# A hybrid decoder layer on one core: the order of the first tiles, of the first input projection weights, and of the last weights

## The chip, the cores and the metric

The kernel runs on one core of one Trainium2 chip. The metric is the device time of one execution in microseconds (us). Engines: TensorE (PE; PEld is its weight load), VectorE (DVE), ScalarE (ACT), GpSimd (POOL), and SyncE (SP), which issues most DMA transfers. Each engine runs its instructions in order; semaphores tie them together.

## The reference

One layer, with S = 512 tokens, D = 1024, feed-forward width 2816, and RMS norms around every sub-layer:

```
h = x + 0.5 * post(swiglu1(pre(x)))            # w_gu 1024 x 5632, w_down 2816 x 1024
z = pre(h) @ W_in + b_in                       # 2304 columns: two mixers' heads
h += post(concat(A, B) @ W_out + b_out)        # A: window + sinks, B: dilated windows
h += 0.5 * post(swiglu2(pre(h)))
h += post(sigmoid(pre(h) @ W_gate) * (p @ W_ple))   # the "gate" stage
```

All is fp32. Token mixing is causal.

## The kernel before, in words

**Operands.** Each fp32 operand is kept as two halves: a high half, which is a ScalarE cast to fp32r (`L197`), and a low half, the source minus the high half (`L198`). A product of two operands is three TensorE products: high x high, high x low, low x high, all issued in `mm` (`L96`). `prep` (`L183`) loads one weight of 128 x 1024 through SP's queue into one of four raw buffers, casts it, and subtracts it. The subtraction runs on `state["lo"]`, which is VectorE or GpSimd.

**Tokens.** The 512 tokens are four tiles t = 0 to 3. `pre` normalises a tile: a Square with its row sum on ScalarE (`L296`), two small GpSimd instructions (`L297`, `L298`), and a scale on VectorE (`L310`). `post` ends a sub-layer with `L320` and `L321` on VectorE. `transpose_x` turns a tile with eight TensorE transposes (`L330`), and makes its high half on ScalarE (`L336`) and its low half on VectorE (`L337`), in two parts of 512 columns each.

**Stages.** ffn1's gate and up products run first; the very first blocks take only the columns of tiles 0 and 1 (256), so that they can start before tiles 2 and 3 are there. Then come ffn1's down products, which use operand slots named "a", "c" and "B" for each block pair, and inside it `e_tile` (a part of the per-layer embedding: products, then a ScalarE copy `L439` into a raw buffer and an SP store `L441`). The seam from ffn1's down products to the attention's input projection has first the four value tiles `v_b(0)` to `v_b(3)` (their weights are "vb"), each with the transposes of the next token tile in its middle, and then the "z" columns. After attention, output projection and ffn2 the gate stage takes tile by tile; its eight weights `("gate", k)` are loaded as slots come free. A tile's columns are computed in parts of 512; the last tile's in 512, 256 and 256. Each part is followed by a chain on ScalarE (`L1124`), VectorE (`L1125`, `L1128`, `L1134`), and after the last part by GpSimd (`L1137`) and the final VectorE step `L1139` with the output's store.

**What sets the order.** TensorE's order is that of the code. At the start the code fixes ScalarE's and VectorE's order as well (`in_order`); elsewhere a scheduler with priorities orders ScalarE, VectorE, GpSimd and SP. `todo` is the list of weights to come, `free` the list of slots, and `release(key)` gives a slot back and lets `pump` prepare the next weight in it.

Of the kernel before, what the change touches and what calls it, by code (L numbers as in the profile page):

```python
# [55 lines left out]
def hybrid_layer(ctx: ExitStack, tc: tile.TileContext, x, p, rel_bias, ffn1_pre_g, ffn1_w_gu, ffn1_w_down,  # L56
# [3 lines left out]
    nc = tc.nc  # L60
# [140 lines left out]
    todo = []  # L201
# [250 lines left out]
            nc.tensor.transpose(PS[:, 0, 0:P], ident, ident)  # L452

    state["first"] = True
    xts = [load_h(0, x)]
    g_pre = bcast(1, ffn1_pre_g)
    xts.append(load_h(1, x))
    warm(24)
    xss = {}
    with in_order():  # L460
        xss[0] = pre(0, xts[0], g_pre, buf("x"))
        prep(todo.pop(0), free.pop(0))
        xss[1] = pre(1, xts[1], g_pre, buf("x"))
        xts.append(load_h(2, x))
        for t in range(2):
            transpose_x(t, xss.pop(t), t)
        prep(todo.pop(0), free.pop(0))
        xss[2] = pre(2, xts[2], g_pre, buf("x"))
    xts.append(load_h(3, x))
    pump()  # L470
    xss[3] = pre(3, xts[3], g_pre, buf("x"))

    def ffn(n, wait_tr, after_first):

# [33 lines left out]
    def down(n, extra, finish, between):  # L508
# [43 lines left out]
        def m7(m, i, e=False):  # L552
            product(C11, i, W[("B" + n, m)], 256, W[("a" + n, m)], 512, False, e)

        def done(m):
            for k in "acB":
                release((k + n, m))
        for fs in ((m3, m2), (m7, m6)):
            for m in range(2):
# [10 lines left out]
        for t in range(2):  # L570
            for f in (m3, m7):
                for m in last:
                    f(m, t, m == NPAIR - 1)
            with tc.high_priority():
                nc.scalar.copy(q[t], C12[t])
            finish(t)
            for m in last:
                m2(m, t, m == NPAIR - 1)
            with tc.high_priority():
                nc.vector.tensor_tensor(q[t], q[t], C21[t], op=ALU.subtract)  # L580
                nc.vector.tensor_tensor(C22[t], C22[t], q[t], op=ALU.add)
        for t in range(2):
            e_tile(n, t)
            if t == 1:
                between(2)
            for m in last:
                m6(m, t, m == NPAIR - 1)
            if t == 1:
                for m in last:
                    done(m)  # L590
            finish(2 + t)
        release(("ple", 0))
        release(("ple", 1))
# [44 lines left out]
    def first_extra():  # L638
        for a in slots1:
            retire(a)  # L640
        assert not todo
        lower(F32R, "heads")
        for j in range(4):
            prep(("vb", j), half_slot(flat(cur["t"]), 1 + j))
        state["lo"] = nc.gpsimd
        todo.extend([("z", f) for f in (QB, KB, QB + 1, KB + 1, QB + 2, KB + 2, QB + 3, KB + 3, KA, VA, 0, 1, 2, 3)])
        todo.extend([("o", f) for f in (6, 7, 0, 1)])

    xss = {}

# [10 lines left out]
    state["first"] = False  # L661


    state["lo"] = nc.gpsimd

    def first(fn):
        def run(*a):
# [37 lines left out]

    v_b(0, lambda: transpose_x(1, xss.pop(1), 1))
    v_b(1, lambda: transpose_x(2, xss.pop(2), 2))
    v_b(2, lambda: transpose_x(3, xss.pop(3), 3))
    v_b(3)
    W.pop(("vb", 0)), W.pop(("vb", 1)), W.pop(("vb", 2)), W.pop(("vb", 3))  # L710
    g_post = bcast(0, attn_post_g)
    g_pre = bcast(1, ffn2_pre_g)
# [394 lines left out]
    for t in range(NT):  # L1107
        ps = flat(slot2(t))
        cols = slice(t * P, (t + 1) * P)
        y, h = ybuf[t], load_h(t)  # L1110
        last = t == NT - 1
        parts = [slice(0, 512), slice(512, 768), slice(768, 1024)] if last else [slice(0, 512), slice(512, 1024)]
        total = None
        for n, c in enumerate(parts):
            o = PS[:, 0, 0:256] if n == 2 else ps[:, c]
            for k in range(NK):
                wh, wl = W[("gate", k)]
                mm(o, XH[:, k, cols], wh[:, c], k == 0, False)
                mm(o, XH[:, k, cols], wl[:, c], False, False)
            if t < 3 and n == 0:  # L1120
                transpose_x(t + 1, xss.pop(t + 1), t + 1)
            for k in range(NK):
                mm(o, XL[:, k, cols], W[("gate", k)][0][:, c], False, k == NK - 1)
            nc.scalar.activation(y[:, c], o, AF.Sigmoid)  # L1124
            nc.vector.tensor_tensor(y[:, c], y[:, c], es[t][:, c], op=ALU.mult)  # L1125
            ms = col()
            if last:
                nc.vector.tensor_tensor_reduce(out=o, in0=y[:, c], in1=y[:, c], scale=1.0 / D,  # L1128
                                               scalar=EPS if n == 0 else total, op0=ALU.mult, op1=ALU.add,
                                               accum_out=ms)  # L1130
            else:
                nc.scalar.activation(o, y[:, c], AF.Square, scale=1.0 / 32.0, accum_out=ms)
                nc.gpsimd.tensor_scalar(ms, ms, EPS if n == 0 else total, None, op0=ALU.add)
            nc.vector.tensor_tensor(y[:, c], y[:, c], g_ple[:, c], op=ALU.mult)  # L1134
            total = ms
        r = col()
        nc.gpsimd.tensor_tensor(r, total, neghalf, op=ALU.pow)  # L1137
        for c in (slice(0, 512), slice(512, 1024)):
            nc.vector.scalar_tensor_tensor(h[:, c], y[:, c], r, h[:, c], op0=ALU.mult, op1=ALU.add)  # L1139
            nc.sync.dma_start(out[t * P:(t + 1) * P, c], h[:, c])  # L1140
# [35 lines left out]
```

## Time and profile before

| | |
|---|---|
| median of three runs | 1014.91 us (1014.45 to 1017.21) |
| the profiled execution, its own time | 1016.56 us |
| its span in the trace | 1014.8 us |
| TensorE busy | 979.2 us (96%) |
| VectorE, ScalarE, GpSimd busy | 630.6, 431.2, 126.6 us |
| TensorE's mean granted clock | 0.986 of full speed |

The span is what the trace covers of the profiled execution; the time beside it is that execution's own. A matmul's end is modelled, so a busy TensorE need not be at its peak. The views are read as: start, duration, engine, line and operation, output from inputs, and in brackets the idle time ahead with what ended it.

### The profile page before, as it was taken

The numbers are of one execution on the slowest core, as the hardware profiler recorded it, in microseconds if no ns is written. First come the engines' busy times: TensorE is split into PE (matmuls) and PEld (weight loads), VectorE is DVE, ScalarE is ACT, GpSimd is POOL, SyncE is SP. The second block draws the span as 40 slices with busy tenths as digits, with TensorE's granted clock in tenths as the row PEclk, the third lists the DMA queues.
The fourth block names the chain that finished last, engine by engine and source line by source line (L and its number), as shares of the span: only waits on it lengthen the run. The fifth ranks groups of instructions, "written<-read, shape, count | busy, mean of one in ns | idle before, by whom it ended". The sixth has DMA issues, their size and how long they took to land.

```text
span 1014.8 us, 12639 instructions
## 1 busy us (share of the span) xinstructions
PE 979.2 (96%) x4769; PEld 823.3 (81%) x4769; DVE 630.6 (62%) x968; ACT 431.2 (42%) x638; POOL 126.6 (12%) x138
## 2 busy tenths in 40 slices
PE   6999999999999998999988999999999999999897
PEld 6987888888887876888877889888888888878786
DVE  5455554554887686277789684545554639776944
ACT  5332222222556463377777354222222225655641
POOL 2000000000000034232232220000000000000411
PEclk7999999999999999999999999999999999999999
DMA  9577768774465567243232365777668544655741
GB/s 276 146 259 239 244 235 292 226 269 159 132 209 187 176 214 230 84 128 111 84 115 63 115 188 183 250 254 252 226 224 275 210 167 153 205 189 190 277 137 63
DMA packets 147992, 193.71 MB, mean 191 GB/s; under 512 B 5993, under 2 KB 112043, under 8 KB 145115
## 3 DMA queue, kind: packets, MB, share of 16 engines
q1 hardware_dynamic: 138779, 141.00, 44.5%
q0 software_dynamic: 9152, 51.91, 14.0%
q8 instruction: 37, 0.61, 0.2%
q14 instruction: 24, 0.20, 0.1%
HBM read 150.91 MB, written 39.35 MB: 187 GB/s over the span
## 4 chain that ended last, share of the span: by engine, by line
PE 50%; DVE 5%; issue 2%; ACT 2%; DMA 1%; POOL 0%; DVEq 0%; POOLq 0%; SPq 0%; ACTq 0%
PE banks L96 48%; DVE hb L863 1%; PE banks L330 1%; DVE fb L899 1%; DVE fb L888 1%; DMA raw<-sums 0%; DVE hb L755 0%; PE banks L908 0%; ACT heads L753 0%; DVE heads L755 0%; ACT heads L762 0%; ACT wr L197 0%; DVE hb L941 0%; PE banks L826 0%; DVE hb L764 0%
## 5 line engine op out<-in xcount | busy, mean ns | idle before, releaser
L96 PE MATMUL banks<-xh,wr 128*128 128x512 f32 (+1 forms) x1024 | 293.4, 367 | 0.1
L96 PE MATMUL banks<-xh,hb 128*128 128x512 f32 (+1 forms) x872 | 254.4, 374 | 0.0
L96 PEld LDWEIGHTS banks<-xh,wr 128*128 128x128 f32 x1024 | 186.7, 191 | 30.0 <-ACT xh L336 0.5
L96 PE MATMUL banks<-xl,wr 128*128 128x512 f32 (+1 forms) x512 | 187.0, 365 | 0.8 <-DVE xl L337 0.8
L96 PEld LDWEIGHTS banks<-xh,hb 128*128 128x128 f32 x872 | 159.9, 188 | 29.5 <-issue 0.6
L96 PE MATMUL banks<-xl,hb 128*128 128x512 f32 (+1 forms) x436 | 161.5, 373 | 0.0
L197 ACT CAST wr<-raw 128x1024 fp32r<-128x1024 f32 x59 | 62.0, 1052 | 142.0 <-PE banks L96 108.5
L197 ACT CAST hb<-raw 128x1024 fp32r<-128x1024 f32 x50 | 52.7, 1053 | 161.6 <-PE banks L96 147.5
L96 PEld LDWEIGHTS banks<-xl,wr 128*128 128x128 f32 x512 | 98.0, 191 | 15.6 <-DVE xl L337 1.1
L388 DVE TENSOR_TENSOR fb<-fb 128x512 f32<-128x512 f32 x110 | 70.1, 687 | 53.6 <-DMA sums<-fb 47.9
L96 PEld LDWEIGHTS banks<-xl,hb 128*128 128x128 f32 x436 | 82.1, 188 | 14.5
L198 DVE TENSOR_TENSOR hb<-raw,hb 128x1024 fp32r<-128x1024 f32 x50 | 60.8, 1221 | 43.6 <-ACT hb L197 43.4
L362 DVE TENSOR_TENSOR hidden<-hidden,banks 128x512 f32<-128x512 f32 x44 | 30.1, 685 | 64.0 <-PE banks L96 63.3
L198 DVE TENSOR_TENSOR wr<-raw,wr 128x1024 fp32r<-128x1024 f32 x41 | 50.0, 1221 | 30.7 <-ACT wr L197 30.6
L297 POOL TENSOR_SCALAR small<-small 128x1 f32<-128x1 f32 x28 | 17.4, 621 | 339.7 <-ACT fb L296 302.9
L147 ACT CAST hb<-raw 128x1024 fp32r<-128x1024 f32 (+1 forms) x37 | 38.5, 1041 | 44.7 <-PE banks L96 41.4
L198 POOL TENSOR_TENSOR wr<-raw,wr 128x1024 fp32r<-128x1024 f32 x18 | 43.9, 2437 | 103.1 <-ACT wr L197 93.1
L148 DVE TENSOR_TENSOR hb<-raw,hb 128x1024 fp32r<-128x1024 f32 (+1 forms) x37 | 44.6, 1206 | 18.0 <-ACT hb L147 17.5
L96 PE MATMUL banks<-hb,wr 128*128 128x512 f32 x210 | 52.3, 390 | 0.7 <-DVE wr L148 0.7
L148 DVE TENSOR_TENSOR wr<-raw,wr 128x1024 fp32r<-128x1024 f32 (+1 forms) x27 | 32.3, 1199 | 33.0 <-ACT wr L147 33.0
L147 ACT CAST wr<-raw 128x1024 fp32r<-128x1024 f32 (+1 forms) x27 | 27.7, 1036 | 52.3 <-PE banks L96 52.3
L96 PE MATMUL banks<-wr,hb 128*128 128x512 f32 x184 | 48.5, 392 | 0.1
(167 smaller groups left out, 1473.8 us busy)
## 6 DMA issues: line engine op xcount, KB each, us to landing
raw<-in_ffn_w_gu_dram SPq DMA_DIRECT2D x88, 512.0 KB, 4.5
sums<-fb POOLq DMA_DIRECT2D x22, 1280.0 KB, 8.1
fb<-in_ffn_w_down_dram POOLq DMA_DIRECT2D x22, 1024.0 KB, 8.5
raw<-sums SPq DMA_DIRECT2D x44, 512.0 KB, 3.5
raw<-in_w_in_dram SPq DMA_DIRECT2D x18, 512.0 KB, 4.4
raw<-in_ffn_w_down_dram SPq DMA_DIRECT2D x24, 256.0 KB, 2.8
raw<-sums SPq DMA_DIRECT2D x22, 256.0 KB, 3.3
fb<-hd SPq DMA_DIRECT2D x11, 512.0 KB, 6.4
```

What stands on the lines that cost most here:

```text
L96: nc.tensor.matmul(o, l, r, start=start, stop=stop, skip_group_check=loose)
L147: nc.scalar.copy(hi, src)
L148: nc.vector.tensor_tensor(lo, src, f32(hi), op=ALU.subtract)
L197: nc.scalar.copy(hi, raw)
L198: state["lo"].tensor_tensor(lo, raw, f32(hi), op=ALU.subtract)
L297: nc.gpsimd.tensor_scalar(ms, ms, 4 * EPS if half else EPS, None, op0=ALU.add)
L330: nc.tensor.transpose(ps[:, k // 4, (k % 4) * P:(k % 4 + 1) * P], xs[:, k * P:(k + 1) * P], ident)
L362: nc.vector.tensor_tensor(h, h, two(ps[:, 1, :]), op=ALU.mult)
L388: nc.vector.tensor_tensor(o[:, i * 512:(i + 1) * 512], x1, x2, op=op)
L863: nc.vector.tensor_tensor(lo, v, f32(hi), op=ALU.subtract)
L888: nc.vector.tensor_tensor_reduce(out=pi, in0=sview(i)[:, :n], in1=back(tb, 0, n), scale=-0.125, scalar=nsink[:, h:h + 1], op0=ALU.add, op1 ...
L899: nc.vector.tensor_scalar(pi, pi, rs[:, i:i + 1], None, op0=ALU.mult)
```

## The change

It has four parts.

1. At the start, x's tiles 0 and 1 are loaded ahead of the gain `bc`, and both are squared ahead of the first weight's cast. Tiles 2 and 3 are loaded ahead of the third weight, tile 3 into a spare `BC` buffer.
2. The list of "z" weights is filled after `v_b(1)` in the code, no longer within ffn1's down stage, and the first three are prepared there with VectorE as `state["lo"]`; GpSimd takes over from the fourth on.
3. The last blocks' "a" slots are released ahead of the e tiles, "c" and "B" after them as before. This holds for ffn1 and ffn2.
4. The last tile's columns are split 512, 384, 128.

```diff
@@ start
-    xts = [load_h(0, x)]
+    xts = [load_h(t, x) for t in range(2)]
     g_pre = bcast(1, ffn1_pre_g)
-    xts.append(load_h(1, x))
     warm(24)
     xss = {}
     with in_order():
-        xss[0] = pre(0, xts[0], g_pre, buf("x"))
+        for t in range(2):
+            xss[t] = pre(t, xts[t], g_pre, buf("x"))
         prep(todo.pop(0), free.pop(0))
-        xss[1] = pre(1, xts[1], g_pre, buf("x"))
-        xts.append(load_h(2, x))
-        for t in range(2):
-            transpose_x(t, xss.pop(t), t)
+        transpose_x(0, xss.pop(0), 0)
+        transpose_x(1, xss.pop(1), 1)
         prep(todo.pop(0), free.pop(0))
+        xts += [load_h(2, x), load_h(3, x, BC[:, 2, :])]
         xss[2] = pre(2, xts[2], g_pre, buf("x"))
-    xts.append(load_h(3, x))
+        prep(todo.pop(0), free.pop(0))
+        xss[3] = pre(3, xts[3], g_pre, buf("x"))
     pump()
-    xss[3] = pre(3, xts[3], g_pre, buf("x"))
@@ down
-        def done(m):
-            for k in "acB":
+        def done(m, kinds="acB"):
+            for k in kinds:
                 release((k + n, m))
...
+        for m in last:
+            release(("a" + n, m))
         for t in range(2):
             e_tile(n, t)
...
                 for m in last:
-                    done(m)
+                    done(m, "cB")
@@ end of ffn1, value products
-        state["lo"] = nc.gpsimd
-        todo.extend([("z", f) for f in (QB, KB, QB + 1, KB + 1, QB + 2, KB + 2, QB + 3, KB + 3, KA, VA, 0, 1, 2, 3)])
-        todo.extend([("o", f) for f in (6, 7, 0, 1)])
...
-    state["lo"] = nc.gpsimd
...
     v_b(1, lambda: transpose_x(2, xss.pop(2), 2))
+    todo.extend([("z", f) for f in (QB, KB, QB + 1, KB + 1, QB + 2, KB + 2, QB + 3, KB + 3, KA, VA, 0, 1, 2, 3)])
+    todo.extend([("o", f) for f in (6, 7, 0, 1)])
+    for _ in range(3):
+        prep(todo.pop(0), free.pop(0))
+    state["lo"] = nc.gpsimd
     v_b(2, lambda: transpose_x(3, xss.pop(3), 3))
     v_b(3)
+    pump()
@@ gate
-        parts = [slice(0, 512), slice(512, 768), slice(768, 1024)] if last else [slice(0, 512), slice(512, 1024)]
+        parts = [slice(0, 512), slice(512, 896), slice(896, 1024)] if last else [slice(0, 512), slice(512, 1024)]
-            o = PS[:, 0, 0:256] if n == 2 else ps[:, c]
+            o = PS[:, 0, 0:128] if n == 2 else ps[:, c]
```

**The start, ScalarE.** From its first Square on, before the change (`fb` are token buffers, `raw` a loaded weight, `wr` and `hb` its operand slots, `banks` the PSUM, `xh` and `xl` the tiles' halves):

```order
L296 ACTIVATE fb,small<-fb 128x1024
L197 CAST wr<-raw 128x1024
L296 ACTIVATE fb,small<-fb 128x1024
L336 CAST xh<-banks 128x4x128 x2
L197 CAST wr<-raw 128x1024
L336 CAST xh<-banks 128x4x128
L197 CAST wr<-raw 128x1024
```

The same place of ScalarE with the change:

```order
L296 ACTIVATE fb,small<-fb 128x1024 x2
L197 CAST wr<-raw 128x1024
L336 CAST xh<-banks 128x4x128 x4
L197 CAST wr<-raw 128x1024
L296 ACTIVATE fb,small<-fb 128x1024
```

The second Square has moved ahead of the first cast, and all four parts of the two tiles' high halves ahead of the second cast. VectorE's order moves in the same way: both L310 ahead of the first L198, four L337 behind it.

**The seam, VectorE.** From the end of ffn1's down stage to the third value tile, before the change (here `bc` holds the gains, and one token tile too):

```order
L310 SCALAR_TENSOR_TENSOR fb<-fb,small,bc 128x1024 x2
L320 TENSOR_TENSOR fb<-banks,bc 128x1024
L321 SCALAR_TENSOR_TENSOR fb<-fb,small 128x1024
L337 TENSOR_TENSOR xl<-banks,xh 128x4x128 x2
L310 SCALAR_TENSOR_TENSOR fb<-fb,small,bc 128x1024
L320 TENSOR_TENSOR fb<-banks,bc 128x1024
L337 TENSOR_TENSOR xl<-banks,xh 128x4x128 x2
L700 TENSOR_TENSOR fb<-banks,fb 128x512
L321 SCALAR_TENSOR_TENSOR bc<-fb,small,bc 128x1024
L704 TENSOR_TENSOR heads<-fb,heads 128x8x64
```

The same place with the change (its L697 and L701 are L700 and L704 of before):

```order
L310 SCALAR_TENSOR_TENSOR fb<-fb,small,bc 128x1024 x2
L320 TENSOR_TENSOR fb<-banks,bc 128x1024
L321 SCALAR_TENSOR_TENSOR fb<-fb,small 128x1024
L337 TENSOR_TENSOR xl<-banks,xh 128x4x128 x2
L198 TENSOR_TENSOR wr<-raw,wr 128x1024
L310 SCALAR_TENSOR_TENSOR fb<-fb,small,bc 128x1024
L320 TENSOR_TENSOR fb<-banks,bc 128x1024
L198 TENSOR_TENSOR wr<-raw,wr 128x1024
L321 SCALAR_TENSOR_TENSOR bc<-fb,small,bc 128x1024
L337 TENSOR_TENSOR xl<-banks,xh 128x4x128 x2
L697 TENSOR_TENSOR fb<-banks,fb 128x512
L701 TENSOR_TENSOR heads<-fb,heads 128x8x64
```

Two low halves, of z1 and z2 (counted from 0), have come in between tile work, and L321 of the last tile stands ahead of the second tile's L337. The low half of z0 has come in too, some rows earlier, ahead of an L321. GpSimd has lost these three, and its order is otherwise the same. On ScalarE the first copy L439 now stands ahead of the Square that it stood behind.

**The gate stage's begin, ScalarE.** Around the two e tiles of ffn2, before the change:

```order
L296 ACTIVATE fb,small<-banks 128x1024
L197 CAST hb<-raw 128x1024
L296 ACTIVATE fb,small<-fb 128x1024
L439 COPY raw<-banks 128x1024
L296 ACTIVATE fb,small<-fb 128x1024
L296 ACTIVATE fb,small<-banks 128x1024
L439 COPY raw<-banks 128x1024
L336 CAST xh<-banks 128x4x128 x2
L197 CAST wr<-raw 128x1024
L296 ACTIVATE fb,small<-banks 128x1024
L296 ACTIVATE fb,small<-fb 128x1024
L197 CAST hb<-raw 128x1024
```

The same place with the change:

```order
L296 ACTIVATE fb,small<-banks 128x1024
L197 CAST hb<-raw 128x1024 x2
L197 CAST wr<-raw 128x1024
L296 ACTIVATE fb,small<-fb 128x1024
L439 COPY raw<-banks 128x1024
L296 ACTIVATE fb,small<-fb 128x1024
L296 ACTIVATE fb,small<-banks 128x1024
L439 COPY raw<-banks 128x1024
L336 CAST xh<-banks 128x4x128 x2
L296 ACTIVATE fb,small<-banks 128x1024
L296 ACTIVATE fb,small<-fb 128x1024
```

Two casts of gate weights have moved up to the first; on VectorE their low halves have moved with them, ahead of the first tile's L310.

## Rows read from the trace of the kernel before

**Rows 1.** Busy time of the engines over the whole span (first part of the page).

```profile
PE 979.2 (96%) x4769; PEld 823.3 (81%) x4769; DVE 630.6 (62%) x968; ACT 431.2 (42%) x638; POOL 126.6 (12%) x138
```

**Rows 2.** Busy time of each engine in three stretches; PEclk is the granted clock.

```profile
23.00:24.00 1.00, 1.00 (x9) 1.00 (x9) 0.23 (x2) 0.51 (x1) 0.71 (x2) 0.80 1.20 290
50.00:100.00 50.00, 50.00 (x247) 42.26 (x245) 27.61 (x42) 13.09 (x16) 4.20 (x6) 1.00 0.76 248
400.00:402.00 2.00, 2.00 (x6) 1.52 (x6) 0.69 (x1) 0.11 (x1) 0.00 (x0) 0.50 0.99 373
```

**Rows 3.** Timeline of the start, 5 to 18.5 us (start, duration, [idle before <-releaser]).

```profile
6.71 1.28 DVE L310 SCALAR_TENSOR_TENSOR fb<-fb,small,bc 128x1024 f32<-128x1024 f32 x1 [5.85 <-DMA bc<-in_ffn_pre_g_dram]
...
9.71 1.04 ACT L197 CAST wr<-raw 128x1024 fp32r<-128x1024 f32 x1 [4.47 <-DMA raw<-in_ffn_w_gu_dram]
...
10.78 1.23 DVE L198 TENSOR_TENSOR wr<-raw,wr 128x1024 fp32r<-128x1024 f32 x1 [2.79 <-ACT wr L197]
...
14.00 1.28 DVE L337 TENSOR_TENSOR xl<-banks,xh 128x512 fp32r<-128x512 f32 x2
...
14.14 1.97 PE L330 MATMUL banks<-ident,fb 128*128 128x128 f32 x8 [5.00 <-DVE fb L310]
...
17.59 0.58 PE L96 MATMUL banks<-xl,wr 128*128 128x256 f32 x1 [0.80 <-DVE xl L337]
```

**Rows 4.** Timeline of the seam, 368 to 407 us, same columns.

```profile
371.30 0.62 PE L96 MATMUL banks<-xh,hb 128*128 128x512 f32 x2
...
373.91 1.00 ACT L439 COPY raw<-banks 128x1024 f32<-128x1024 f32 x1
...
380.28 0.38 SPq L196 DMA_DIRECT2D raw<-in_w_in_dram  x1
...
381.98 3.50 DVE L310 SCALAR_TENSOR_TENSOR fb<-fb,small,bc 128x1024 f32<-128x1024 f32 x1 [0.98 <-POOL small L298]
...
382.00 2.40 POOL L198 TENSOR_TENSOR wr<-raw,wr 128x1024 fp32r<-128x1024 f32 x1
...
385.88 1.05 ACT L197 CAST wr<-raw 128x1024 fp32r<-128x1024 f32 x1 [2.94 <-DMA raw<-in_w_in_dram]
...
388.19 4.00 PE L96 MATMUL banks<-heads,xh 128*128 128x512 f32 x16 [0.99 <-DVE xl L337]
...
391.54 1.05 ACT L197 CAST wr<-raw 128x1024 fp32r<-128x1024 f32 x1 [3.64 <-DMA raw<-in_w_in_dram]
...
396.38 1.28 DVE L310 SCALAR_TENSOR_TENSOR fb<-bc,small 128x1024 f32<-128x1024 f32 x1 [0.77 <-POOL small L298]
...
398.32 5.54 PE L96 MATMUL banks<-heads,xh 128*128 128x512 f32 x16 [3.38 <-DVE xl L337]
```

**Rows 5.** Timeline of the gate's first tile, 945 to 967 us, same columns.

```profile
950.77 1.27 DVE L310 SCALAR_TENSOR_TENSOR fb<-fb,small,bc 128x1024 f32<-128x1024 f32 x1
...
953.66 1.03 PE L330 MATMUL banks<-ident,fb 128*128 128x128 f32 x8
...
960.53 0.50 PE L96 MATMUL banks<-hb,xh 128*128 128x512 f32 x1 [0.50 <-ACT hb L197]
...
963.20 0.50 PE L96 MATMUL banks<-hb,xh 128*128 128x512 f32 x1 [2.17 <-DVE hb L198]
...
963.54 1.03 PE L330 MATMUL banks<-ident,fb 128*128 128x128 f32 x8
```

**Rows 6.** Timeline of 128-column products and of the tail, same columns.

```profile
458.06 0.22 PE L96 MATMUL banks<-heads,hb 128*128 128x128 f32 x1
...
458.22 0.45 PE L96 MATMUL banks<-xh,wr 128*128 128x512 f32 x1
...
1001.48 1.34 PE L96 MATMUL banks<-gates,xh 128*128 128x256 f32 x10
...
1004.30 1.31 PE L96 MATMUL banks<-gates,xh 128*128 128x256 f32 x10
...
1009.61 1.41 DVE L1139 SCALAR_TENSOR_TENSOR fb<-fb,small 128x512 f32<-128x512 f32 x2 [0.44 <-POOL small L1137]
```

## The prediction

> **What bounds the kernel now.** I read the page's first part, then the windows, then the timeline of every stretch in which TensorE's busy time falls short, engine by engine. TensorE is busy 979.2 of 1014.8 us [rows 1]; in the long stages it has no gap at all at full clock (50.00 of 50 us, [rows 2]). So no edit that only frees another engine's time is worth anything unless it ends one of TensorE's waits, makes TensorE do less, or gives it its clock sooner. The 35.6 us of gaps sit in a few places, and the change touches four: the start, the seam from ffn1's down stage to the value products, the gate's first tile, and the last tile's tail. The sum below is made against the profiled execution, 1016.56 us (span 1014.8 and 1.76 around it); the median of the three runs shown is 1014.91, so 1.65 comes off at the end.
>
> **Start: -3.7.** Now the first product that reads a low half starts at 17.59, held by VectorE's third L337 [rows 3]. That one is the last of a chain: the gain `bc` lets L310 of tile 0 start at 6.71, but L310 of tile 1 stands behind the first low half L198 (10.78) and, on ScalarE, the Square of tile 1 behind the first cast, which waits for the weight's DMA until 9.71. TensorE's transposes of tile 1 follow at 14.14, after 5.00 of waiting. After the change both Squares are done before that cast. The cast itself stays at 9.71: x0, x1, gain and g0 are still the first four loads. The gain is the third now, not the second: it lands no sooner than 6.71 and no later than g0's 9.71; I take the middle, 8.2. Two L310 (1.28 each) end at about 10.8, L198 of g0 (from 10.8, when the cast ends, 1.23) at 12.0, three L337 (0.64 each, half of the 1.28 for two) at 13.9. That is the new start of the low products, 3.7 before 17.59. With the gain at 9.71, two L310 end at 12.3, L198 at 13.5, L337 at 15.4: -2.2. The clock makes the other bound. It comes up in slice 23 to 24 (0.80, [rows 2]), and if it comes up no earlier, the 3.7 us are run at 1.2 GHz and are worth half, -1.9; if it rises as much earlier as the products do, all 3.7, and with the gain landing at 6.71 up to -5. I take 3.7, since the products run without a break from 17.59 on and before them the engine waited. The two x loads that now stand ahead of g1 in SP's queue delay g1 by one load: it lies under g0's and u0's 48 short products. If that cover is gone the price is the length of one load, about 2.4 us (g0, the fourth load, was there at 9.71), inside the range.
>
> **Seam: -3.4.** The change text says that weights wait for the value products, but by the order the loads of the first z weights stand where they did in SP's queue. What moves is two things. On ScalarE the copy of the first e tile (L439) now goes ahead of a Square that waits for VectorE. TensorE's e products end at 371.9 (371.30 and 0.62, [rows 4]), so the copy can run at 372.0, not 373.91: 1.9 earlier. The raw buffer that it feeds from is freed by its store, and the load of z2, at 380.28, waits for that: 378.4; z2's cast, which waits for this DMA, goes from 385.88 to 384.0, z3's from 391.54 to 389.6. And the low halves of z0, z1 and z2 go from GpSimd (2.40 each) to VectorE (1.22). That adds 3 x 1.22 = 3.7 us to VectorE ahead of tile work, and it takes away what GpSimd did to VectorE: L310 at 381.98 took 3.50 beside GpSimd's 2.40 of low half, against 1.28 [rows 4], so one such meeting cost 2.2.
> At the second value tile: z2's cast ends 385.05, L198 1.22, L321 1.28 (the same size as L310), first L337 0.64, which is 388.2, against 388.19 now: nothing gained or lost, any gain upstream ends in this wait. At the third: z3's low half stays on GpSimd ahead of the norm of tile 3, so the chain from z3's cast (391.54) over L310 (396.38) to the products (398.32) keeps its 6.8 us and starts 1.9 earlier: 396.4, so -1.9. The wait there falls from 3.38 to 1.5. After the 3.38 TensorE's clock was 0.50 in 400 to 402 [rows 2], that is 1.2 GHz, and sixteen products took 5.54 against 4.00 for the same sixteen at 388.19: with the shorter wait I take 4.00, another -1.5. Bounds: if z2 lands no earlier, nothing (0); if the second wait (0.99) and the third both vanish with the clock's 1.5, -0.99 - 3.38 - 1.5 = -5.9. I take -3.4.
>
> **Gate: -1.8.** The earlier release of the "a" slots brings the last three gate weights forward on ScalarE and VectorE. Two more L198 (2 x 1.22 = 2.44) now stand ahead of L310 of tile 0: 950.77 becomes 953.2, its end 954.5, and the transposes that wait for it start at 954.5 in place of 953.66: +0.85. In exchange the two waits of the first gate tile end, 0.50 for a cast and 2.17 for a low half [rows 5], since their weight is ready before the tile: -2.67. The next transposes (963.54) come 1.8 earlier. Bounds: nothing, if the weight still comes last; -2.67, if the two L198 find a hole.
>
> **Tail: +0.5.** The last tile's columns go from 512/256/256 to 512/384/128. 24 products of 256 took 2.82 (1001.48 to 1004.30, [rows 6]); 384 columns are 1.5 x 2.82 = 4.2. For 128 columns the nearest row is a pair that took 0.16, 458.06 to 458.22: 24 x 0.08 = 1.9, against 1.4 for half of 2.82. So TensorE ends at 1001.48 + 4.2 + 1.9 = 1007.6 instead of 1004.30 + 2.82 = 1007.1. What follows (ScalarE, VectorE and GpSimd up to L1139 at 1009.61) took 2.5. It works on half the columns now, but behind the longer chain of the 384 before it on the same VectorE; I let the two cancel, so +0.5. Bounds: half of 2.82 for the last part gives 0, and up to 0.3 less if the shorter steps show; the whole of 2.82 gives +1.4.
> The Trainium skill has a rule against such a split: "TensorE: Matmul & The Clock Gate", section "LDWEIGHTS (loading the stationary operand)", gives a weight load P/1.2 ns, with P the columns of the weight, however short the product is; an estimate from it is 107 ns for 128 columns, 24 x 0.107 = 2.6 us, and the sum would be 0.7 higher. The same page's "Back-to-back issue gap" has about 81 ns for a sustained product of 128 columns. The pair above, at 0.08 us, agrees with the second and not with the first as a pace; two products are little to go by.
>
> **Sum.** -3.7 - 3.4 - 1.8 + 0.5 = -8.4: 1016.56 becomes 1008.2, and against the median of 1014.91 it is 1006.5. The lows of the terms add up to -13.9, the highs to -0.5. "The same" is within 0.3% (3.0 us), about what a measurement of this kernel can tell from no change: 1011.9 to 1018.0.
>
> **The rivals.**
> (1) The seam gives nothing: the low halves that VectorE takes over (3.7 us) stand in order ahead of L321 and L337, the very instructions that TensorE waits for, and use up what z2's earlier landing gives. For it: the second value tile already comes out at no gain. Against it: VectorE's own L310 was held by 2.2 in the same stretch. Time 1006.5 + 3.4 = 1009.9.
> The Trainium skill, "SBUF — State Buffer", section "Who interferes with whom", calls the port that VectorE and GpSimd share an exclusive lock; the 3.50 of L310 agrees, and by that rule the move should help, though no run yet shows a stretch without it.
> (2) The start's gain is given back: the weights, not the tiles, come last, and TensorE runs into g1 or u1, or it stays at 1.2 GHz to 23.4 and then waits. For it: casts wait for DMA at 9.71 already, and the load queue is full in this stretch. Against: 48 short products cover each later weight. Time 1006.5 + 3.7 = 1010.2.
> (3) Both: 1013.6, no measurable change.
> (4) The other side. VectorE runs in order, and the low halves of z1 and z2 now make it wait for their weights' DMA, where GpSimd could wait apart. Behind z2's stand L321 and the L337 of tile 1, for which TensorE waits. Each us by which z2's cast comes later than 384.0 is lost one for one; the other terms and the 0.3% use up 8.4 + 3.0 = 11.4, so it decides from a cast at 395.4 on, and a cast at 397 gives 1006.5 + 13 = 1019.5. Against it: z2's load is issued at 380.28 now and its cast ran 5.6 later.
>
> **How the numbers follow.** The forecast as summed, 1006.5, gets 0.63; (1) 0.15; (2) 0.10; (3) 0.08; (4) 0.04. The first three are faster, 0.88; the third is the same, 0.08; the last slower, 0.04. The range: with the terms' lows not all at once, 1006.5 - 4 = 1002.5 below; above it takes in (1) and (2), 1011.
>
> **What would show it.** Start: the first low product near 13.9 and full clock by about 20. Seam: z2's cast near 384.0, L310 of tile 2 at 1.28 and not 3.50, the second value tile still at about 388 less what the start gave, the third after a wait of 1.5 with 4.00 for its sixteen products. (All later places come earlier by what the stages before them gave.) Gate: no wait inside the first tile, and transposes 0.85 late ahead of it. Tail: 1.9 us for the last 24 products. The prediction is wrong if casts of z1 or z2 wait longer than now with VectorE behind them, if the clock in the seam still falls to 0.50, or if the gate weights bring a new wait ahead of the first transposes of more than 2 us.

## The result and the profile after

The changed kernel takes 1005.91 us (median of 6 runs, 1004.67 to 1008.54), the kernel before 1015.92 in the same set (6 runs, 1014.45 to 1017.47). The ratio is 0.9902, 95% interval 0.9885 to 0.9919: some 10 us faster. The profiled execution took 1006.38 us, its span is 1004.6, 10.2 less than the span before. The forecast was 1006.5, 8.4 less than 1014.91, the median of before that it started from; between the two medians here it is 10.0.

The first part of the page of the changed kernel, the busy time of the engines:

```profile
PE 977.9 (97%) x4769; PEld 822.9 (82%) x4769; DVE 628.8 (63%) x971; ACT 432.3 (43%) x638; POOL 120.1 (12%) x135
```

TensorE works about as long as before (977.9 against 979.2, [rows 1]); what went is nearly all waiting. (A line number behind the changed start can differ by a few: L535 after is L536 of before.) Where it went is read from the places of [rows 3] to [rows 6]. First the start, timeline of the changed kernel (start, duration, idle before and its releaser in brackets):

```profile
7.99 2.48 DVE L310 SCALAR_TENSOR_TENSOR fb<-fb,small,bc 128x1024 f32<-128x1024 f32 x2 [7.13 <-DMA bc<-in_ffn_pre_g_dram]
...
9.33 3.68 PE L330 MATMUL banks<-ident,fb 128*128 128x128 f32 x16 [3.44 <-DVE fb L310]
...
9.84 1.04 ACT L197 CAST wr<-raw 128x1024 fp32r<-128x1024 f32 x1 [3.18 <-DMA raw<-in_ffn_w_gu_dram]
...
10.92 1.22 DVE L198 TENSOR_TENSOR wr<-raw,wr 128x1024 fp32r<-128x1024 f32 x1 [0.45 <-ACT wr L197]
...
12.06 2.47 DVE L337 TENSOR_TENSOR xl<-banks,xh 128x512 fp32r<-128x512 f32 x4
...
13.99 0.58 PE L96 MATMUL banks<-xl,wr 128*128 128x256 f32 x1 [0.55 <-DVE xl L337]
```

Both L310 run in one go at 7.99, the first weight's cast starts at 9.84, four L337 follow L198 without a break, and the first low product stands at 13.99 in place of 17.59. Its clock, in the windows view (PEclk is the third number from the right):

```profile
8.00:9.00 1.00, 0.00 (x0) 0.00 (x0) 1.00 (x1) 0.00 (x0) 0.00 (x0) 0.64 1.17 336
...
18.00:19.00 1.00, 1.00 (x8) 1.00 (x8) 1.00 (x1) 0.85 (x3) 0.80 (x1) 0.74 1.20 260
```

It stood at 1.00 after the idle transposes, fell to 0.50 within slice 8 to 9, in the break behind them, and came up again in slice 18 to 19; before, in 23 to 24 [rows 2]. The seam, the same view as [rows 4]:

```profile
367.93 1.02 ACT L439 COPY raw<-banks 128x1024 f32<-128x1024 f32 x1 [1.72 <-PE banks L96]
...
373.63 0.38 SPq L196 DMA_DIRECT2D raw<-in_w_in_dram  x1
...
375.44 4.00 PE L96 MATMUL banks<-heads,xh 128*128 128x512 f32 x16
...
377.82 1.05 ACT L197 CAST wr<-raw 128x1024 fp32r<-128x1024 f32 x1
...
377.89 1.29 DVE L310 SCALAR_TENSOR_TENSOR fb<-fb,small,bc 128x1024 f32<-128x1024 f32 x1 [0.77 <-POOL small L298]
...
379.04 0.38 SPq L196 DMA_DIRECT2D raw<-in_w_in_dram  x1
...
383.29 4.00 PE L96 MATMUL banks<-heads,xh 128*128 128x512 f32 x16 [1.10 <-DVE xl L337]
...
384.55 1.06 ACT L197 CAST wr<-raw 128x1024 fp32r<-128x1024 f32 x1 [3.56 <-DMA raw<-in_w_in_dram]
...
385.68 2.39 POOL L198 TENSOR_TENSOR wr<-raw,wr 128x1024 fp32r<-128x1024 f32 x1 [6.08 <-ACT wr L197]
...
388.16 0.55 POOL L297 TENSOR_SCALAR small<-small 128x1 f32<-128x1 f32 x1
...
389.39 1.28 DVE L310 SCALAR_TENSOR_TENSOR fb<-bc,small 128x1024 f32<-128x1024 f32 x1 [0.77 <-POOL small L298]
...
391.33 3.99 PE L96 MATMUL banks<-heads,xh 128*128 128x512 f32 x16 [1.30 <-DVE xl L337]
```

The copy L439 now starts at 367.93. Taking off the 4.09 us by which the e products ahead of it start earlier (364.95 after, 369.04 before), it is 1.9 earlier. z2's cast (377.82) has no DMA to wait for any more. L310 of tile 2 takes 1.29, not 3.50. The first value tile starts without a wait, the second still waits 1.10, the third 1.30 in place of 3.38, and its sixteen products take 3.99. Two rows of the trace before, for what follows on the seam, are the first value tile, with its wait, and the load of z3 (379.04 after):

```profile
380.46 4.00 PE L96 MATMUL banks<-heads,xh 128*128 128x512 f32 x16 [0.85 <-DVE xl L337]
...
387.11 0.38 SPq L196 DMA_DIRECT2D raw<-in_w_in_dram  x1
```

The gate's first tile, answering to [rows 5]:

```profile
945.42 1.06 PE L330 MATMUL banks<-ident,fb 128*128 128x128 f32 x8 [0.60 <-issue]
...
952.68 1.04 PE L330 MATMUL banks<-ident,fb 128*128 128x128 f32 x8
```

From the first transposes to the next it takes 7.26 us in place of 9.88; ahead of the first there is now a gap of 0.77 (the product before them ends its issue at 944.65), of which 0.60 is shown as issue. Inside the tile one short wait is new, 0.29 for L337 at 948.85. The tail, answering to [rows 6]:

```profile
990.61 1.91 PE L96 MATMUL banks<-gates,xh 128*128 128x384 f32 x10
...
994.80 1.22 PE L96 MATMUL banks<-gates,xh 128*128 128x128 f32 x10
...
997.31 0.28 PE L96 MATMUL banks<-wr,xl 128*128 128x128 f32 x1
...
999.44 1.41 DVE L1142 SCALAR_TENSOR_TENSOR fb<-fb,small 128x512 f32<-128x512 f32 x2 [0.44 <-POOL small L1140]
```

The last 24 products, of 128 columns, run from 994.80 to about 997.42. L1142 is the line that was L1139.

This table is worked out from the traces of all runs (us). E is the start of the first e product of ffn1's down stage, "clock up" the slice in which the clock rises for good at the start, "seam" from E to the start of the fourth value tile, "gate" from the first gate tile's leading transposes to the next, "tail" from the last tile's first product to the start of the last VectorE step. A time is the median of its runs, or one execution in the rows "last part of 64" and "gain second"; all other columns are read from one profiled execution. The times come from four sets, in which the kernel before had medians of 1015.92, 1015.74 (the three single parts and no split), 1016.13 (from halves on GpSimd to 41 idle transposes) and 1015.87 (the last four rows).

| run | time | first low product | clock up | E | seam | gate | tail |
|---|---|---|---|---|---|---|---|
| before | 1015.92 | 17.59 | 23-24 | 369.04 | 37.39 | 9.88 | 13.70 |
| changed | 1005.91 | 13.99 | 18-19 | 364.95 | 32.96 | 7.26 | 14.40 |
| start alone | 1010.04 | 13.83 | 17-18 | 364.21 | 36.73 | 10.07 | 13.71 |
| seam alone | 1012.49 | 17.43 | 23-24 | 368.80 | 33.02 | 9.89 | 13.70 |
| release in ffn2 alone | 1013.38 | 17.52 | 21-22 | 367.94 | 37.45 | 7.26 | 13.71 |
| no split | 1005.71 | 13.60 | 12 | 363.52 | 33.18 | 7.26 | 13.71 |
| halves on GpSimd | 1007.40 | 14.49 | 13-14 | 363.13 | 35.65 | 7.26 | 13.71 |
| one half on VectorE | 1005.03 | 13.70 | 13-14 | 363.89 | 32.63 | 7.26 | 13.71 |
| four halves | 1002.87 | 14.12 | 12-13 | 363.98 | 31.62 | 7.25 | 13.70 |
| 41 idle transposes | 1006.27 | 13.83 | before 8 | 364.98 | 33.20 | 7.25 | 13.70 |
| last part of 64 | 1006.91 | 13.74 | 12-13 | 363.97 | 35.03 | 7.24 | 14.80 |
| gain second | 1007.88 | 14.30 | 18 | 366.30 | 33.26 | 7.25 | 13.71 |
| changed, again | 1005.74 | 14.24 | 13-14 | 363.25 | 32.81 | 7.25 | 14.40 |
| four halves, again | 1005.39 | 14.04 | 17 | 364.29 | 31.63 | 7.26 | 13.71 |

### The profile page after: what moved, and what is told of

Same layout as the page of the kernel before. It is cut to its first block, busy times and chain, and to the rows that moved or that the text cites. A ratio compares the mean times of both kernels' runs of the same rounds, so it can differ in the third digit from the quotient of the medians.

```text
span 1004.6 us, 12638 instructions
## 1 busy us (share of the span) xinstructions
PE 977.9 (97%) x4769; PEld 822.9 (82%) x4769; DVE 628.8 (63%) x971; ACT 432.3 (43%) x638; POOL 120.1 (12%) x135
## 4 chain that ended last, share of the span: by engine, by line
PE 84%; DVE 7%; issue 3%; DMA 2%; ACT 2%; POOL 1%; SPq 0%; DVEq 0%; POOLq 0%; ACTq 0%
PE banks L96 82%; DVE hb L866 1%; PE banks L330 1%; DMA raw<-in_ffn_w_gu_dram 1%; DVE fb L902 1%; DVE fb L891 1%; DMA raw<-in_w_in_dram 1%; DMA ed<-raw 0%; PE banks L911 0%; DVE hb L758 0%; DMA raw<-sums 0%; DVE xl L148 0%; ACT heads L756 0%; ACT wr L197 0%; DVE heads L758 0%
## 5 line engine op out<-in xcount | busy, mean ns | idle before, releaser
L96 PE MATMUL banks<-xh,wr 128*128 128x512 f32 (+1 forms) x1024 | 292.9, 366 | 0.0
L96 PE MATMUL banks<-xh,hb 128*128 128x512 f32 (+1 forms) x872 | 254.3, 374 | 0.0
L96 PEld LDWEIGHTS banks<-xh,wr 128*128 128x128 f32 x1024 | 186.2, 191 | 29.8 <-ACT xh L336 0.3
L96 PE MATMUL banks<-xl,wr 128*128 128x512 f32 (+1 forms) x512 | 186.8, 365 | 0.6 <-DVE xl L337 0.6
L96 PEld LDWEIGHTS banks<-xh,hb 128*128 128x128 f32 x872 | 159.9, 188 | 29.5 <-issue 0.6
L96 PE MATMUL banks<-xl,hb 128*128 128x512 f32 (+1 forms) x436 | 161.5, 373 | 0.0
L96 PEld LDWEIGHTS banks<-xl,wr 128*128 128x128 f32 x512 | 97.7, 191 | 15.4 <-DVE xl L337 0.8
L96 PEld LDWEIGHTS banks<-xl,hb 128*128 128x128 f32 x436 | 82.1, 188 | 14.5
L198 DVE TENSOR_TENSOR hb<-raw,hb 128x1024 fp32r<-128x1024 f32 x50 | 61.0, 1221 | 41.9 <-ACT hb L197 41.6
L198 DVE TENSOR_TENSOR wr<-raw,wr 128x1024 fp32r<-128x1024 f32 x44 | 53.6, 1220 | 26.2 <-ACT wr L197 26.0
L297 POOL TENSOR_SCALAR small<-small 128x1 f32<-128x1 f32 x28 | 16.1, 575 | 334.4 <-ACT fb L296 298.5
L96 PE MATMUL banks<-hb,wr 128*128 128x512 f32 x210 | 52.2, 390 | 0.7 <-DVE wr L148 0.7
L198 POOL TENSOR_TENSOR wr<-raw,wr 128x1024 fp32r<-128x1024 f32 x15 | 36.6, 2442 | 103.5 <-ACT wr L197 103.5
L96 PE MATMUL banks<-wr,hb 128*128 128x512 f32 x184 | 48.5, 392 | 0.1
```

The costliest lines, as they stand in the source:

```text
L96: nc.tensor.matmul(o, l, r, start=start, stop=stop, skip_group_check=loose)
L198: state["lo"].tensor_tensor(lo, raw, f32(hi), op=ALU.subtract)
L297: nc.gpsimd.tensor_scalar(ms, ms, 4 * EPS if half else EPS, None, op0=ALU.add)
```

## The experiments

**Each part alone.** Three kernels are the kernel before with one part of the change. The start alone:

```diff
-    xts = [load_h(0, x)]
+    xts = [load_h(t, x) for t in range(2)]
     g_pre = bcast(1, ffn1_pre_g)
...
+        for t in range(2):
+            xss[t] = pre(t, xts[t], g_pre, buf("x"))
         prep(todo.pop(0), free.pop(0))
```

> The kernel before with the new start alone. My theory: each part's gain is its own, and the start's is whole: about 4 us below before (1015.9 becomes 1012), with the first low product at 14.0 in place of 17.6 and the clock at its upper level by 19. Rival (the start's gain is given back later): the first product is early, but a wait appears behind it before 300 us and the time stays within 1 us of before.

Measured: 1010.04 us, ratio 0.9939 (0.9919 to 0.996), 5.7 below before. The seam of this run is still 36.73 and its gate 10.07, so this is the start and nothing behind it. The rival falls: no new wait follows it before 300 us.

The seam alone:

```diff
-        state["lo"] = nc.gpsimd
-        todo.extend([("z", f) for f in (QB, KB, QB + 1, KB + 1, QB + 2, KB + 2, QB + 3, KB + 3, KA, VA, 0, 1, 2, 3)])
...
     v_b(1, lambda: transpose_x(2, xss.pop(2), 2))
+    todo.extend([("z", f) for f in (QB, KB, QB + 1, KB + 1, QB + 2, KB + 2, QB + 3, KB + 3, KA, VA, 0, 1, 2, 3)])
...
+    for _ in range(3):
+        prep(todo.pop(0), free.pop(0))
+    state["lo"] = nc.gpsimd
```

> The kernel before with the later list of z weights and VectorE for the first three low halves alone. My theory: 4.4 us below before, the wait ahead of the third value tile 1.3 in place of 3.4 and its sixteen products 4.0 in place of 5.5. Rival (the seam's gain came from the early start or from the release of the slots): within 1 us of before, the wait still above 3.

Measured: 1012.49 us, ratio 0.9966 (0.9952 to 0.9979), 3.2 below. Third wait 1.37, sixteen products 4.00. Neither the start nor the release is needed.

The release alone:

```diff
+        if n == "2":
+            for m in last:
+                release(("a" + n, m))
         for t in range(2):
             e_tile(n, t)
...
-                    done(m)
+                    done(m, "cB" if n == "2" else "acB")
```

> The kernel before with the earlier release of the a slots in ffn2 alone. My theory: 1.9 us below before (waits of 0.5 and 2.2 inside the first gate tile gone, 0.85 more ahead of its transposes). Rival (the gain of the gate needs the other parts): within 0.5 us.

Measured: 1013.38 us, ratio 0.9971 (0.9959 to 0.9983), 2.4 below; in the trace the gate falls from 9.88 to 7.26 and a gap of 0.60 stands ahead of its transposes. The three parts add up to 11 with an uncertainty of 1 to 2 each, the whole change gave 10 and pays 0.7 at the tail: no sign that the parts need or disturb each other.

**The tail's split.** The changed kernel with the old columns:

```diff
-        parts = [slice(0, 512), slice(512, 896), slice(896, 1024)] if last else [slice(0, 512), slice(512, 1024)]
+        parts = [slice(0, 512), slice(512, 768), slice(768, 1024)] if last else [slice(0, 512), slice(512, 1024)]
```

> The changed kernel with the last tile in 512, 256 and 256 columns again. My theory, from the trace of the changed kernel: the 24 products of 128 columns took 2.6 and not 1.9, so the end comes 0.7 us sooner than in the changed kernel (1005.9 becomes 1005.2; the trace must show it, the time is too coarse). Rival (the shorter chain pays for the dearer products): no sooner, the distance from the last part's begin to L1142 then makes up for it.

Measured: 1005.71 us, ratio 0.9894 (0.9876 to 0.9912); the time does not tell the two apart. The trace does (timeline of this run's tail):

```profile
991.05 1.31 PE L96 MATMUL banks<-gates,xh 128*128 128x256 f32 x10
...
996.36 1.42 DVE L1142 SCALAR_TENSOR_TENSOR fb<-fb,small 128x512 f32<-128x512 f32 x2 [0.44 <-POOL small L1140]
```

From the last tile's first product it is 13.71 to the last VectorE step, against 14.40 with the split: 0.69, and 13.70 or 13.71 in all eleven traces with 512, 256 and 256 columns. Whether it is the columns or the weights that a short product waits for, the next one asks, with parts of 512, 448 and 64:

```diff
-        parts = [slice(0, 512), slice(512, 896), slice(896, 1024)] if last else [slice(0, 512), slice(512, 1024)]
+        parts = [slice(0, 512), slice(512, 960), slice(960, 1024)] if last else [slice(0, 512), slice(512, 1024)]
```

> The changed kernel with the last tile in 512, 448 and 64 columns. My theory (a product this short lasts as long as its weight load, 0.11 us): the last 24 products take 2.6 us again, half the columns of the changed kernel's notwithstanding. Rival (per column, 0.02 us for 128): 1.3 us, or with a pace of 0.04, 1.0.

One execution, 1006.91 us. Its tail:

```profile
990.74 2.19 PE L96 MATMUL banks<-gates,xh 128*128 128x448 f32 x10
...
995.61 1.20 PE L96 MATMUL banks<-gates,xh 128*128 128x64 f32 x10
...
998.09 0.28 PE L96 MATMUL banks<-wr,xl 128*128 128x64 f32 x1
...
999.97 1.41 DVE L1142 SCALAR_TENSOR_TENSOR fb<-fb,small 128x512 f32<-128x512 f32 x2 [0.44 <-POOL small L1140]
```

24 products of 64 columns, 995.61 to 998.20: 2.6 us again, 0.108 each. Between 128 and 64 the columns do not count any more; the rival falls. The Trainium skill, "TensorE: Matmul & The Clock Gate", section "LDWEIGHTS (loading the stationary operand)", gives a weight load P/1.2 ns; an estimate from it is 107 for 128 weight columns, and both runs agree with it. The 81 ns that the same page of the Trainium skill has under "Back-to-back issue gap" are not reached here: 0.109 with 128 columns.

**Which engine makes the low halves.** The next three runs are without the split. With the first three halves on GpSimd again:

```diff
+    state["lo"] = nc.gpsimd
     todo.extend([("z", f) for f in (QB, KB, QB + 1, KB + 1, QB + 2, KB + 2, QB + 3, KB + 3, KA, VA, 0, 1, 2, 3)])
```

> The run without the split (512, 256, 256 columns; 1005.7), with the first three z weights' low halves on GpSimd again, their place in the code unchanged. By the order, the copy L439 is then behind the Square again. My theory: the engine of these halves is the whole seam, so 4.4 us slower (1010.1): L321 held at above 2.5, the wait ahead of the third value tile above 3 and its sixteen products above 5. Rival (the later list is what counts): within 1 us of 1005.7.

Measured: 1007.40 us, ratio 0.9913 (0.9894 to 0.9931). Its seam:

```profile
364.17 2.74 DVE L321 SCALAR_TENSOR_TENSOR fb<-fb,small 128x1024 f32<-128x1024 f32 x1
...
375.71 3.50 DVE L310 SCALAR_TENSOR_TENSOR fb<-fb,small,bc 128x1024 f32<-128x1024 f32 x1 [0.98 <-POOL small L298]
...
381.18 4.00 PE L96 MATMUL banks<-heads,xh 128*128 128x512 f32 x16 [0.24 <-DVE xl L337]
...
390.67 5.53 PE L96 MATMUL banks<-heads,xh 128*128 128x512 f32 x16 [2.76 <-DVE xl L337]
```

L321 is held to 2.74 and L310 to 3.50 again, the third wait is 2.76 and the clock falls (5.53). So far as forecast, but the time is 1.7 above the run without the split, not 4.4, and the seam is 35.65, 2.5 above that run's 33.18, where before it was 4.2 above. The other 1.7 (1.1, measured against the start alone) come with the later list or the release in ffn1, which I did not part. My theory was too simple.

The trace says more. Of the 2.5, 1.5 are the clock, and that fall is not the engine's alone: the run with a last part of 64, whose three halves are on VectorE, has it too (seam 35.03). The other 0.9 is z3's cast, 20.76 after E here and 19.83 without the split; the third tile starts 6.78 behind the one and 6.77 behind the other, whether L310 took 3.50 or 1.28. And the second tile comes at 18.06 after E here, at 18.34 without the split. So at the second tile the prediction's first rival has it right: z2's low half (1.22) and L321 (1.28), which stand ahead of its L337 on VectorE with the change, use up what the freed L310 gives.

With only z0's low half on VectorE:

```diff
-    for _ in range(3):
+    prep(todo.pop(0), free.pop(0))
+    state["lo"] = nc.gpsimd
+    for _ in range(2):
         prep(todo.pop(0), free.pop(0))
-    state["lo"] = nc.gpsimd
```

> The run without the split, with only z0's low half on VectorE, z1's and z2's on GpSimd; the copy L439 stays ahead of the Square. My theory (z0's half alone held up VectorE ahead of the first value tile; z1's and z2's give nothing, or cost VectorE what they save): no wait ahead of the first value tile, the second tile's wait within 0.5 of 1.1, the third's near 1.5, time within 1 us of 1005.7. Rival (all three halves count, each by the 1.2 to 2.2 us for which GpSimd held VectorE): second and third tile later by 1 to 3 us, the clock falls again, 1007 to 1010.

Measured: 1005.03 us, ratio 0.9885 (0.9866 to 0.9903), seam 32.63, no worse than with three. But neither theory has it right:

```profile
378.66 3.07 POOL L198 TENSOR_TENSOR wr<-raw,wr 128x1024 fp32r<-128x1024 f32 x1
...
379.41 3.40 DVE L321 SCALAR_TENSOR_TENSOR bc<-fb,small,bc 128x1024 f32<-128x1024 f32 x1
...
383.46 4.00 PE L96 MATMUL banks<-heads,xh 128*128 128x512 f32 x16 [2.35 <-DVE xl L337]
...
390.04 3.90 PE L96 MATMUL banks<-heads,xh 128*128 128x512 f32 x16
```

GpSimd's low half of z2, begun at 378.66, holds L321 to 3.40, and the second wait grows from 1.10 to 2.35; the third is gone. z0's half on VectorE is enough for the seam; z1's and z2's only move a wait from the third tile to the second. With z0's half the copy L439 stands ahead of the Square, in every run that has it there, and behind it in every other; no run parts the two.

With four on VectorE:

```diff
-    for _ in range(3):
+    for _ in range(4):
         prep(todo.pop(0), free.pop(0))
```

> The run without the split, with a fourth low half (z3's) on VectorE: GpSimd's two norm steps of the last token tile no longer stand behind 2.39 of low half. My theory: the third value tile comes 1.3 us earlier, its wait near 0: 1004.4. Rival (VectorE's own 1.22 and its wait for z3's DMA take the place): wait still 1.0 or more, 1005.7 or later.

Measured: 1002.87 us, ratio 0.9873 (0.9852 to 0.9893):

```profile
384.46 1.23 DVE L198 TENSOR_TENSOR wr<-raw,wr 128x1024 fp32r<-128x1024 f32 x1 [1.01 <-ACT wr L197]
...
385.57 0.22 POOL L297 TENSOR_SCALAR small<-small 128x1 f32<-128x1 f32 x1 [6.94 <-ACT fb L296]
...
386.47 1.28 DVE L310 SCALAR_TENSOR_TENSOR fb<-bc,small 128x1024 f32<-128x1024 f32 x1 [0.78 <-POOL small L298]
...
389.01 4.00 PE L96 MATMUL banks<-heads,xh 128*128 128x512 f32 x16
```

The low half of z3 (384.46) takes 1.23 on VectorE, and the third value tile starts with no wait: seam 31.62, 1.6 less than with three. The gain is not that VectorE is held less, since L310 of the last tile took 1.28 already. It is GpSimd's own queue: the norm step L297 of that tile now starts at 385.57, as soon as the Square's row sum is there; in the changed kernel the sum was there at 386.65, and L297 (388.16) stood behind z3's low half (385.68 and 2.39). The time is 2.8 lower, more than that, so it stood again on one chip beside the changed kernel.

> The changed kernel again, to stand on one chip beside the next run: 1005.9, and in its profile a clock at the start that rises anywhere between 12 and 19 us.

> The kernel without the split and with four low halves on VectorE again. If the trace's 0.7 at the tail and 1.4 at the seam are real: 2.1 us below the changed kernel on this chip, about 1003.8. If its earlier 1002.9 was the clock's luck alone: within 1 us of the changed kernel.

Measured: the changed kernel 1005.74 (ratio 0.9905, 0.9888 to 0.9922), four halves without the split 1005.39 (0.9898, 0.9881 to 0.9915). The intervals overlap. In the traces seam (31.63 against 32.81) and tail (13.71 against 14.40) are 1.9 better, as before; but in this pair the clock rose at 17 in the one and at 13 to 14 in the other, and E is 1.0 later. It is better in its rows in both profiles; that it is faster is not shown by times.

**The clock at the start.** The same kernel without the split, with more idle transposes:

```diff
-    warm(24)
+    warm(41)
```

> The run without the split, with 41 in place of 24 idle transposes at the start, which fill TensorE's wait from 5.9 to 9.3 us. My theory: the clock rises after TensorE has worked without a long break, so it rises ahead of or soon after the first product near 13 and not between 15 and 18.5: 1 to 2.8 us less, 1003 to 1004.7. Rival (what counts are the products themselves): the clock rises as late as before, no change from 1005.7.

Measured: 1006.27 us, ratio 0.9904 (0.9882 to 0.9925). Two windows and TensorE's timeline of this run:

```profile
10.00:12.00 2.00, 1.37 (x11) 0.89 (x9) 1.57 (x3) 2.00 (x4) 0.00 (x0) 1.00 1.09 380
...
25.00:50.00 25.00, 23.48 (x196) 23.04 (x195) 13.80 (x17) 12.43 (x15) 0.00 (x0) 1.00 0.62 172
```

```profile
29.68 0.65 PE L330 MATMUL banks<-ident,fb 128*128 128x128 f32 x4 [0.44 <-DVE xl L337]
...
31.41 0.66 PE L330 MATMUL banks<-ident,fb 128*128 128x128 f32 x4 [1.08 <-DVE xl L337]
```

The theory was right on the clock (it stays at 1.00 through the first products) and wrong on the time. TensorE now comes to the transposes of tile 3 too soon: they wait 0.44 and 1.08 for L337, which stands on VectorE behind low halves whose weights come from the DMA, and 25 to 50 us holds 23.48 of busy time instead of 25. E is 364.98, with the clock at 18 it was 364.95. The rival of the prediction in which the start's gain is given back does exist, as a wait of about 1 us. The clock alone does not set it: of the six other runs with the clock up between 12 and 14, three have this wait (no split, one half on VectorE, last part of 64: 0.91 to 1.18) and three have not.

The gain loaded second again:

```diff
-    xts = [load_h(t, x) for t in range(2)]
+    xts = [load_h(0, x)]
     g_pre = bcast(1, ffn1_pre_g)
+    xts.append(load_h(1, x))
```

> The run without the split, with the gain loaded second again (x0, gain, x1, g0); all else of the new start kept. My theory: with both tiles scaled before g0's cast ends, the chain from that cast (9.7 to 9.9) sets the first low product, so it stays at 13.6 to 14.1. Rival (the gain's place in the queue counts): earlier by up to 1.2 us, the gain then landing near 6.7.

One execution: 1007.88 us, the first low product at 14.30, no earlier. For the first low product the gain's place does not count. E is 366.30 here, later than in all others of the new start. The clock rose at 18, as in the changed kernel, but transposes wait for L337 once more:

```profile
32.34 1.25 PE L330 MATMUL banks<-ident,fb 128*128 128x128 f32 x8 [1.05 <-DVE xl L337]
```

That is 1.05 of the 1.35 by which E is behind the changed kernel's. Why it waits here, with the clock so late, stays open.

## Why the prediction was right, step by step

**What bounds the kernel** was right: the time left by the ends of TensorE's waits, at the four places and at one more (below).

**Start, forecast -3.7.** The first low product came at 13.99 (forecast 13.9), the gain at 7.99 (8.2), the cast at 9.84 (9.71). E is 4.09 earlier in the pair of profiles; over the nine profiles of the new start with 24 idle transposes and the gain third it is 363.1 to 365.0, against 367.9 to 369.0 with the old. The products are worth 3.6; the clock, which rose some 4.9 earlier (in 18 to 19 for 23 to 24), more than they did, fits the rest. The start alone was 5.7 faster in time, 4.1 to 8.2 by its interval: the size holds within that.

**Seam, forecast -3.4, measured -4.43** (37.39 to 32.96). The chain to the third value tile was right and its first term too small. The forecast had it start 6.8 behind z3's cast; in all eleven traces in which it waits it starts 6.77 to 6.80 behind that cast. The cast was to come 1.9 earlier, as much as the copy L439. It came 2.9 earlier (391.54 - 369.04 = 22.50 after E, now 384.55 - 364.95 = 19.60), and with the clock's 1.5 as forecast that is the 4.4. The gain grows on the way: L439 1.9 earlier, z2's load 2.56 (380.28, now 373.63, less 4.09), and z3's load, which the trace shows released by the second e tile's store, 3.98 (387.11 and 379.04); that load then took 1.1 longer to its cast. I had carried the 1.9 through.
The sentence that the second value tile gains nothing failed too: it comes 0.8 earlier after E, and the third wait, 2.1 shorter, makes up the rest of the 2.9. The wait of 0.85 ahead of the first value tile is gone. With the start alone and with the halves on GpSimd it is 0.49, with L321 held to 2.74 in both, so at most this 0.49 is due to the low halves; what took the other 0.36 is not shown. z2's cast came 4.0 earlier, not 1.9 (377.82 + 4.09 = 381.9 against 385.88), and did not count at the second tile.
The port rule of the Trainium skill ("SBUF — State Buffer", "Who interferes with whom") stands: with GpSimd's low half beside them, L310 and L321 took 2.74, 3.40 and 3.50, and without it none above 1.29 in the seam. But these rows do not price the seam. L321's 2.74 is ahead of the Square behind which the copy L439 stood, so it is in the chain, by an amount that no run parts from the new order; L310's 3.50 sets the second tile alone.

**Gate, forecast -1.8, measured -1.85:** 2.62 of waiting gone, 0.77 of delay ahead of the first transposes (forecast 2.67 and 0.85). The 2.62 is from transposes to transposes, with the new wait of 0.29 in it. The 0.77 is one profile's: in seven of the eleven traces with the release it is 0.76 or 0.77, in one 0.86, and in three 1.27 to 1.43, among them the changed kernel's second profile:

```profile
944.06 1.06 PE L330 MATMUL banks<-ident,fb 128*128 128x128 f32 x8 [1.10 <-ACT fb L296]
```

There the gate is worth 1.35 and not 1.85; the table's column begins at the transposes and does not show it.

**Tail, forecast +0.5, measured +0.70.** The size of the last part was wrong: I took 0.08 us a product from one pair, 24 x 0.08 = 1.9, and it took 2.6. The chain behind it gave 0.5 back (2.0 from the last product to the last step, not 2.5), which I had let cancel. The rule that I set aside for that pair was the right one; two products in the midst of longer ones say nothing on the pace of 24. The weight loads around that pair had the pace already, 0.11 apart in the trace before:

```profile
458.06 0.19 PEld L96 LDWEIGHTS banks<-hb 128*128 128x128 f32 x1
458.17 0.19 PEld L96 LDWEIGHTS banks<-xh,wr 128*128 128x128 f32 x1
```

**What the sum left out:** 0.5 us in ffn2's down stage, where a wait of L96 for VectorE (L536) was 1.7 and is 1.2. It varies between 1.0 and 1.7 among the fourteen traces, with no part of the change at it.
In all: -4.1 - 4.4 - 0.5 - 1.85 + 0.7 = -10.2, the difference of the spans. The slower rival did not come: z2's cast came earlier, not later. Part of the agreement is luck: the profiles behind these terms differ among themselves by 1.9 in E and 0.5 ahead of the gate.

## What to carry to other kernels

A bulk instruction on GpSimd is not free when VectorE has short work on the critical path: look for VectorE instructions at two or three times their usual length and at what GpSimd runs beside them, and for short GpSimd steps that stand behind it. Whether such an instruction costs time is read from the chain that ends last: here it was a weight's DMA, which started when a copy's store had freed its buffer. When a column split is made to shorten a tail, price its short products by the weight load and not by their columns: 24 of them took 2.8 us with 256 columns and 2.6 with 128 and with 64. And a gain that ends in a wait is best followed to every later reader of the same wait, not only to the one nearest to the moved instruction.

## What the hardware showed that I had not expected

The clock's rise is not fixed by the program. With one start and one order of instructions up to there it rose at 12 in one run (below) and at 18 to 19 in the changed kernel's first profile, and with the old start between 21 and 24.

```profile
12.00:13.00 1.00, 0.70 (x4) 0.29 (x2) 1.00 (x3) 0.99 (x3) 0.00 (x0) 1.00 0.97 380
```

PEclk 0.50 is 1.2 GHz and 1.00 is 2.4. What TensorE did before: idle transposes up to about 6 us, a break of 2.9 in that run and 3.4 in the changed kernel, in or after which the clock fell, then transposes and products. With 41 idle transposes, and a break of 1.03 behind them, the clock was at its upper level by 8 us and did not fall.

Its fall is not fixed by the program either. In attention, 120 to 130 us behind the fourth value tile, the same stretch ran at 0.83 in the kernel before and at 1.00 with the start alone:

```profile
526.43:536.43 10.00, 7.98 (x44) 7.49 (x44) 8.68 (x28) 6.49 (x17) 0.01 (x1) 0.83 0.19 56
```

```profile
520.94:530.94 10.00, 7.98 (x53) 7.26 (x53) 9.72 (x34) 7.56 (x19) 1.38 (x1) 1.00 0.19 57
```

And in the run with a last part of 64 columns the third value tile's wait of 1.84 was followed by the lower clock, while 2.35 ahead of the second tile was not (above):

```profile
390.88 5.54 PE L96 MATMUL banks<-heads,xh 128*128 128x512 f32 x16 [1.84 <-DVE xl L337]
```

Single executions of one kernel differ by 2 to 6 us, in part for such reasons, which is why differences of one or two are read from the rows and not from the times.
